# Output products of a hybrid mixer, on one Trainium2 core, written as twelve jobs of seven products

## The chip, the cores and the metric

The kernel is one program on one core of a Trainium2 chip (trn2). The metric is the device time of one execution in microseconds (us). Most executions of it agree within 0.3%, so differences of about 0.2% need several runs of each kernel.

## The reference

One layer of a decoder trunk on a sequence of 1024 tokens of width 1024, in fp32. What matters here is the middle of it, with what stands on both sides:

```python
h = x
h = h + 0.5 * swiglu(rms_norm(h, ffn1_norm), ffn1_w_in, ffn1_w_out)
h = h + hybrid_mixer(rms_norm(h, mix_norm), ...)
h = h + 0.5 * swiglu(rms_norm(h, ffn2_norm), ffn2_w_in, ffn2_w_out)
hn = rms_norm(h, ple_norm)
h = h + sigmoid(hn @ ple_w_gate) * (p @ ple_w_proj)      # then a last rms_norm

def hybrid_mixer(u, ...):
    # projections of u; branch A: gated linear attention (GLA), 4 heads of 256 columns
    y_gla = o @ gla_w_out                 # o: 1024 x 1024
    # branch B: indexer, top-k, latent attention, 8 heads of 128 columns
    y_dsa = od @ dsa_w_out                # od: 1024 x 1024
    return (sigmoid(g_A) * y_gla + sigmoid(g_B) * y_dsa) @ w_out
```

The change concerns the three products of 1024x1024 by 1024x1024 in the last lines: o by gla_w_out (wgo in the kernel), od by dsa_w_out (wdo), and the gated sum by w_out (wmo).

## The kernel before

Activations lie transposed: a tile is 128 columns of the model by 1024 tokens, and a 1024-wide matrix is 8 such tiles. An fp32 product is made of three passes on rounded values: every operand is split into a high part (a copy into the rounded type, on ScalarE, ACT) and a rest (value minus high part, on VectorE, DVE), and high by high, high by rest and rest by high are summed in PSUM. A matmul instruction takes a 128x128 block of weights and 512 tokens.

Two ways of multiplying stand in the kernel. The **plain** one is `dense` and `column` (L121 to L140): one output tile of 128 columns is 8 (blocks of the sum) x 2 (halves of the tokens) x 3 = 48 matmuls. The **seven products** (`_Job`, `seven`, L252) serve both feed-forwards: the weight block of a job and the tokens are cut in two each way, and seven products of sums of blocks (numbers 1, 5, 6, 3, 7, 2, 4 in the order SEVEN) take the place of eight. For 8 tiles of input and 2 of output, which is a job with 4 blocks of the sum (KP = 4), that is 7 x 4 x 3 = 84 matmuls where the plain way takes 96. It needs sums of weight blocks (`sums7`, four subtractions or additions of 128x512 for each job, on GpSimd, POOL, or on DVE for the jobs in the list `crowded`), the split of each of the seven weights (`headrest`, called by `split7`: 128x512, high part on ACT, rest on DVE), and operands that are sums of blocks of the tokens (tiles `xo`, read as pieces `b` of 128x512 from memory, high part on ACT, rest on DVE: `part`). PSUM has three banks for the seven products (table BANK: 1, 6, 7, 4 in the first, 5, 3 in the second, 2 in the third), so a product must wait until the product before it in its bank has been drained by `done`.

What sets the order: the feed-forwards issue everything through `_InOrder` engines, that is, in the order in which the Python code writes it. All else (the GLA, the top-k, the latent attention and `mixer_out`) is placed by a scheduler that sorts instructions for each engine. DMAs stand in the order of one queue, that of SyncE (SP).

A **transition** is a place in a feed-forward where the input of the jobs changes (from the gate and up projections to the output projection, and from one window of the output projection to the next): all 28 operand tiles (7 products by 4 blocks) are then read and split anew (`feed`, L398) while the last jobs of the old input and the first of the new are running.

Around the change:

- GLA (L1200 to L1211) ends with its output tiles `o`, split by ACT and POOL into a high part and a rest that go to memory as `d_og`, 2 tiles for each 128 columns, 4 DMAs for a head.
- Latent attention (L1336 to L1346) ends every block of 128 queries and pair of heads in PSUM (`pv`); ACT copies the high part (`oh`), DVE makes the rest (`ol`), and four DMAs of 64 KB store them as `d_od`. The gate projections are woven in between.
- `mixer_out` (L1362) reads them back (`reload`, 16 DMAs of 512 KB for each of the two) and makes 3 x 8 plain output tiles, 24 x 48 = 1152 matmuls: for each of wgo a gate multiplication (`y`), for each of wdo a gate multiplication, an addition to `y` on POOL and a split, for each of wmo the addition to the residual (`hm`, L1386).
- The second feed-forward (`ffn`, L301) then starts with one plain job (4 blocks of 24 matmuls, of which the first 72 matmuls are one run) whose operands are `hm` times a gain, split on ACT and DVE (`tile_alone`), and with the sum of squares of `hm` (`square`: ACT `sq`, DVE `ss`), from which `pstat` (a matmul with ones), `r` and the row factor `R` follow.

## Time and profile before

| | |
|---|---|
| median of 3 runs | 2715.18 us (2714.36 to 2715.75) |
| the profiled execution | 2716.55 us, span of its instructions 2714.8 us |
| mean granted TensorE clock | 0.979 of full speed |
| TensorE (PE) busy | 2599.2 us, 96% of the span, 12114 matmuls |
| VectorE (DVE) busy | 1809.0 us, 67% |
| ScalarE (ACT) busy | 1143.9 us, 42% |
| GpSimd (POOL) busy | 761.4 us, 28% |
| from the last latent matmul to the last matmul of `mixer_out` | 1647.3 to 1898.3 us of the span |

A matmul of 128x512 is shown with some 0.39 us, but matmuls overlap: what counts is the distance between two starts. The views name tiles without their numbers, `pd<-xo,w` is a matmul of the seven-product kind (or of the plain job of a feed-forward), `pd<-xh,wh` one of the plain kind. In the square brackets of a timeline stand the idle time of the engine just before the group and what ended it.

### The profile page before, as it was taken

The numbers are of one execution on the slowest core, as the hardware profiler recorded it, in microseconds if no ns is written. First come the engines' busy times: TensorE is split into PE (matmuls) and PEld (weight loads), VectorE is DVE, ScalarE is ACT, GpSimd is POOL, SyncE is SP. The second block draws the span as 40 slices with busy tenths as digits, with TensorE's granted clock in tenths as the row PEclk, the third lists the DMA queues.
The fourth block names the chain that finished last, engine by engine and source line by source line (L and its number), as shares of the span: only waits on it lengthen the run. The fifth ranks groups of instructions, "written<-read, shape, count | busy, mean of one in ns | idle before, by whom it ended". The sixth has DMA issues, their size and how long they took to land. (4 is left out here: it accounts for less than half of the span.)

```text
span 2714.8 us, 33415 instructions
## 1 busy us (share of the span) xinstructions
PE 2599.2 (96%) x12114; PEld 2156.9 (79%) x12114; DVE 1809.0 (67%) x3157; ACT 1143.9 (42%) x1814; POOL 761.4 (28%) x533
## 2 busy tenths in 40 slices
PE   8999999999999999898999999999799999999997
PEld 6788887777888878787778887887588888777786
DVE  7866658768568999986256663232876655866865
ACT  6443334435445555432257662121543333443542
POOL 1555553222002132223222220110165555322200
PEclk9999999999999999898999999999899999999998
DMA  3343336434323233231432266332134333643322
GB/s 133 132 148 129 116 124 243 168 115 143 95 78 109 98 120 140 78 132 63 168 105 98 91 211 232 111 116 86 47 133 150 130 112 124 244 167 114 119 94 85
DMA packets 129253, 346.21 MB, mean 128 GB/s; under 512 B 14488, under 2 KB 34880, under 8 KB 129088
## 3 DMA queue, kind: packets, MB, share of 16 engines
q1 hardware_dynamic: 129088, 344.08, 36.5%
q8 instruction: 95, 1.56, 0.2%
q14 instruction: 70, 0.57, 0.1%
HBM read 230.75 MB, written 110.65 MB: 126 GB/s over the span
## 5 line engine op out<-in xcount | busy, mean ns | idle before, releaser
L1399 PE MATMUL pd<-xo,w 128*128 128x512 f32 x5580 | 1296.2, 394 | 55.0 <-DVE xo L1399 14.7
L1399 PEld LDWEIGHTS pd<-xo,w 128*128 128x128 f32 x5580 | 1058.0, 190 | 291.7 <-DVE xo L1399 23.4
L139 PE MATMUL pd<-xh,wh 128*128 128x512 f32 x1346 | 533.7, 398 | 19.1 <-DVE z L1064 18.6
L139 PE MATMUL pd<-xl,wh 128*128 128x512 f32 x1346 | 531.0, 396 | 0.0
L139 PE MATMUL pd<-xh,wl 128*128 128x512 f32 x1346 | 451.2, 395 | 0.0
L1399 DVE TENSOR_TENSOR w<-wr,w 128x512 fp32r<-128x512 f32 (+1 forms) x272 | 213.3, 786 | 190.9 <-ACT w L1399 190.8
L139 PEld LDWEIGHTS pd<-xh,wh 128*128 128x128 f32 x1346 | 255.1, 190 | 73.4 <-DVE z L1064 17.6
L139 PEld LDWEIGHTS pd<-xl,wh 128*128 128x128 f32 x1346 | 255.4, 190 | 51.8 <-issue 1.0
L139 PEld LDWEIGHTS pd<-xh,wl 128*128 128x128 f32 x1346 | 254.2, 190 | 52.9 <-issue 0.5
L118 DVE TENSOR_TENSOR wl<-wr,wh 128x1024 fp32r<-128x1024 f32 (+1 forms) x106 | 125.4, 1183 | 213.0 <-PE pd L139 104.4
L1399 ACT ACTIVATE w<-wr 128x512 fp32r<-128x512 f32 (+1 forms) x272 | 161.9, 613 | 140.7 <-PE pd L1399 116.3
L117 ACT ACTIVATE wh<-wr 128x1024 fp32r<-128x1024 f32 (+1 forms) x106 | 101.8, 961 | 261.9 <-PE pd L139 226.8
L1399 POOL TENSOR_TENSOR g<-g,R 128x512 f32<-128x512 f32 x78 | 115.8, 1485 | 306.1 <-ACT g L1399 302.6
L1399 DVE TENSOR_TENSOR w<-ws,w 128x512 fp32r<-128x512 f32 (+1 forms) x195 | 177.4, 910 | 5.5 <-ACT w L1399 4.9
L1399 DVE TENSOR_TENSOR hr<-hr,pd 128x512 f32<-128x512 f32 x160 | 109.2, 683 | 102.4 <-PE pd L1399 102.3
L1399 ACT ACTIVATE w<-ws 128x512 fp32r<-128x512 f32 (+1 forms) x195 | 119.0, 611 | 97.9 <-PE pd L1399 73.2
L1399 POOL TENSOR_TENSOR ws<-wr 128x512 f32<-128x512 f32 (+1 forms) x59 | 97.5, 1653 | 209.6 <-DVE w L1399 209.6
L1399 ACT ACTIVATE g<-g 128x512 f32<-128x512 f32 (+1 forms) x85 | 55.1, 648 | 219.3 <-DVE g L1399 219.3
L1399 ACT ACTIVATE g<-pd 128x512 f32<-128x512 f32 x82 | 49.1, 598 | 169.7 <-PE pd L1399 169.7
L169 POOL TENSOR_TENSOR r<-r,mhalf 128x8 f32<-128x8 f32 (+1 forms) x11 | 17.2, 1565 | 366.5 <-DVE r L168 360.8
L1399 DVE TENSOR_TENSOR xo<-b,xo 128x512 fp32r<-128x512 f32 x138 | 109.7, 832 | 0.5 <-ACT xo L1399 0.5
L1133 POOL TENSOR_TENSOR g_e<-g_b 128x512 f32<-128x512 f32 x28 | 35.5, 1268 | 252.1 <-DVE g_b L1107 204.0
(272 smaller groups left out, 3417.7 us busy)
## 6 DMA issues: line engine op xcount, KB each, us to landing
wr<-wm SPq DMA_DIRECT2D x54, 512.0 KB, 3.4
wr<-w1i SPq DMA_DIRECT2D x44, 512.0 KB, 4.1
d_hid<-u SPq DMA_DIRECT2D x44, 512.0 KB, 4.8
d_ts<-ts SPq DMA_DIRECT2D x44, 512.0 KB, 2.6
wr<-w2i SPq DMA_DIRECT2D x44, 512.0 KB, 4.2
b<-d_ts SPq DMA_DIRECT2D x72, 256.0 KB, 3.1
b<-d_hid SPq DMA_DIRECT2D x66, 256.0 KB, 4.3
d_sp<-m SPq DMA_DIRECT2D x32, 256.0 KB, 3.1
```

Of the source, the lines that this page charges most:

```text
L117: (ac or nc.scalar).activation(wh, raw, AF.Copy)
L118: (eng or self.weng).tensor_tensor(wl, raw, F(wh), op=ALU.subtract)
L139: te.matmul(ps[h], ww[:, ks], v[:, h * 512:h * 512 + 512], start=first and ww is wh and v is xh, stop=last and ww is wl)
L169: nc.gpsimd.tensor_tensor(r, r, self.mhalf[:, :nb], op=ALU.pow)
L1133: nc.gpsimd.tensor_tensor(ev[:, :, :m], ref, bv[:, :, :m], op=ALU.subtract)
L1399: ins = getattr(self.eng, name)(*args, **kw)
```

## The change

`mixer_out` becomes twelve jobs of seven products, 4 for each of wgo, wdo, wmo, each with KP = 4 and two output tiles; they stand in one list with the jobs of the second feed-forward, use its buffers (they are reserved once for both) and are issued in written order. 12 x 84 = 1008 matmuls take the place of 1152.

- **What feeds them.** GLA stores seven pieces of 128x512 for each head (blocks and differences of blocks; 4 subtractions of 128x512 on POOL, 7 DMAs of 256 KB) and no longer splits its output. Latent attention stores, for the first four query blocks, ACT's copy `olo`, and for the last four one tile `pc` of five 128x128 blocks (2 copies on ACT, 4 subtractions of 128x128 on POOL, one DMA), both single-buffered; the DVE instruction `ol` is gone. The gated sum of jobs 4 and 5 is stored as finished pieces (`sums`), that of jobs 6 and 7 is made in place (`made`).
- **When.** `feed` is now a method: at most 6 pieces are asked for ahead. The first 12 of the 28 operand tiles of wgo are made before job 0, then 4 for each product. The feeds of wdo and wmo are spread over 13 products of jobs 3 and 4, and of jobs 7 and 8.
- **Into the feed-forward.** `ffn` is a generator; `tile_alone` and `square` of tiles 0 to 5 run inside job 11 (the last of wmo). The blocks of the plain job go through the queue of ready weights.
- **`crowded`.** The lists are given by hand now. In both feed-forwards the sums of weights of the jobs around the second and the third transition (jobs NF + 3, NF + 4, NF + 7, NF + 8) move from POOL to DVE; of the new jobs, 3, 4, 7, 8 and 11 have them on DVE.

The core of the diff:

```diff
-        self.next = (plain, 0)
+        self.next = (0, 0)
...
     def sums7(self, job, step, eng=None):
-        if job >= len(self.jobs):
+        if job >= len(self.jobs) or self.jobs[job].plain:
             return
...
-            self.ready.append(self.headrest(j.w[SEVEN[q]], j.n))
+            self.ready.append(self.headrest(j.blk[BLOCKS[q]] if j.plain else j.w[SEVEN[q]], j.n))
...
-        self.crowded = (NF - 1, NF)
...
             tile_alone(j)
             if plain == 1:
                 square(j, hs[j])
+                if j % 2:
+                    yield
...
-        hs = self.mixer_out(d, mg, xp, yp, hp)
...
-        self.start(self.products(a, "w2"), 1)
+        jobs = [_Job(a[w][n], KP) for w in ("wgo", "wdo", "wmo") for n in range(KP)]
+        jb = len(jobs)
+        self.start(jobs + self.products(a, "w2", 1),
+                   [3, 4, 7, 8, 11] + [jb + NF + i for i in (-1, 0, 3, 4, 7, 8)])
...
-                oh = u("e", dtype=FR)
-                ol = u("e", dtype=FR)
-                nc.scalar.activation(oh, o, AF.Copy)
-                nc.gpsimd.tensor_tensor(ol, o, F(oh), op=ALU.subtract)
-                nc.sync.dma_start(d["og"][2 * j], F(oh))
-                nc.sync.dma_start(d["og"][2 * j + 1], F(ol))
+                os[half] = o
+            ta, tb = u("e"), u("e")
+            for t, x, y in ((ta[:, lo], os[0][:, hi], os[0][:, lo]), (tb[:, hi], os[1][:, hi], os[0][:, hi]),
+                            (tb[:, lo], os[1][:, hi], ta[:, lo]), (ta[:, hi], os[1][:, lo], tb[:, lo])):
+                nc.gpsimd.tensor_tensor(t, x, y, op=ALU.subtract)
+            for p, t in ((1, os[0][:, lo]), (5, ta[:, lo]), (6, tb[:, lo]), (3, os[1][:, hi]), (7, tb[:, hi]),
+                         (2, os[1][:, lo]), (4, ta[:, hi])):
+                nc.sync.dma_start(d["og"][h][:, PIECE[p], :], t)
...
-                nc.scalar.activation(oh, pv[:, :256], AF.Copy)
-                nc.vector.tensor_tensor(ol, pv[:, :256], F(oh), op=ALU.subtract)
+                    nc.scalar.activation(ohi, pair_of[:, 0, :], AF.Copy)
+                    nc.scalar.activation(pc[:, 2, :], pair_of[:, 1, :], AF.Copy)
+                    for t, x, y in ((0, ohi, olo[:, 0, cs]), (1, pc[:, 2, :], pc[:, 0, :]), (3, pc[:, 2, :], ohi),
+                                    (4, olo[:, 1, cs], pc[:, 1, :])):
+                        nc.gpsimd.tensor_tensor(pc[:, t, :], x, y, op=ALU.subtract)
+                    nc.sync.dma_start(out[:, 1:6, cs], pc)
...
+        count = next(feeds[0])
+        for q in range(4):
+            self.sums7(0, q, self.ve if q else None)
+        while count < upto[0][0]:
+            count = next(feeds[0])
+        for q in range(AHEAD):
+            self.split7()
+        for job in range(12):
+            j.ops, j.done = ops[w], (gla_out, latent_out, added)[w](n)
+            for q in self.seven(job):
+                if n in (0, 3) and wi == (w if n == 0 else w + 1):
+                    turn += 1
+                    want = upto[wi][min(turn, len(upto[wi]) - 1)] if wi else min(28, 12 + 4 * turn)
+                    while count < min(28, want):
+                        count = next(feeds[wi])
...
+                if job == 11 and q in (0, 3, 5):
+                    next(ffn)
+        next(ffn)
```

Where the order moves, at three places. First the queue of SP between the latent attention and the output products. `d_od` is the attention's output in memory, `g` a gate, `xh`, `xl` the stored halves, `b` a piece of GLA's output `d_og`. Before:

```order
L1345 DMA d_od_147<-oh 128x128
L1345 DMA d_od_149<-oh 128x128
L1346 DMA d_od_148<-ol 128x128
L1346 DMA d_od_150<-ol 128x128
L1368 DMA g<-d_gate_103 128x1024
L1368 DMA g<-d_gate_104 128x1024
L1368 DMA g<-d_gate_105 128x1024
L1357 DMA xh<-d_od_135 128x1024
L1358 DMA xl<-d_od_136 128x1024
```

After:

```order
L1376 DMA d_od_194<-pc 128x5x128 x4
L313 DMA b<-d_og_187 128x512
L313 DMA b<-d_og_188 128x512
L313 DMA b<-d_og_189 128x512
L313 DMA b<-d_og_190 128x512
L313 DMA b<-d_og_187 128x512
L313 DMA b<-d_og_188 128x512
L313 DMA b<-d_og_189 128x512
L1393 DMA g<-d_gate_103 128x1024
L1393 DMA g<-d_gate_104 128x1024
L313 DMA b<-d_og_190 128x512
```

Before, GLA's output had been read by then, and the attention's output follows its last store; now GLA's output is read only behind the last store of the attention.

Second, DVE at the start of the output products. `w` is the rest of a weight, `xo` the rest of an operand tile, `b` the piece that it comes from, `y` an output. After (before, this place holds the rests `wl` of plain weights, each followed by two gate multiplications):

```order
L1547 TENSOR_TENSOR wr<-wr 128x512
L1547 TENSOR_TENSOR xo<-b,xo 128x512 x12
L1547 TENSOR_TENSOR w<-wr,w 128x512
L1547 TENSOR_TENSOR w<-ws,w 128x512 x3
L1547 TENSOR_TENSOR w<-wr,w 128x512
L1547 TENSOR_TENSOR xo<-b,xo 128x512 x4
L1547 TENSOR_TENSOR w<-wr,w 128x512
L1547 TENSOR_TENSOR xo<-b,xo 128x512 x4
L1547 TENSOR_TENSOR w<-wr,w 128x512
L1547 TENSOR_TENSOR xo<-b,xo 128x512 x4
```

Twelve operand tiles stand ahead of the first weight, and twelve more between the weights of the first products.

Third, DVE at the end of the output products. `hm` is the residual tile that the last products are added to, `xo<-hm,gains` the operand of the plain job of the feed-forward, `ss` the sum of squares. Before:

```order
L1386 TENSOR_TENSOR hm_15050<-pd,hm_15050 128x512 x2
L1386 TENSOR_TENSOR hm_15110<-pd,hm_15110 128x512 x2
L1386 TENSOR_TENSOR hm_15170<-pd,hm_15170 128x512 x2
L1399 TENSOR_TENSOR ss<-ss,sq 128x1024
L1399 SCALAR_TENSOR_TENSOR xo<-hm_14870,gains,xo 128x512 x2
L1399 TENSOR_TENSOR ss<-ss,sq 128x1024
L1399 SCALAR_TENSOR_TENSOR xo<-hm_14930,gains,xo 128x512 x2
L1399 TENSOR_TENSOR ss<-ss,sq 128x1024
```

After:

```order
L1547 TENSOR_TENSOR hm<-hm,pd 128x512
L1547 TENSOR_TENSOR w<-wr,w 128x512
L1547 SCALAR_TENSOR_TENSOR xo<-hm,gains,xo 128x512 x4
L1547 TENSOR_TENSOR ss<-ss,sq 128x1024
L1547 TENSOR_TENSOR hm<-hm,pd 128x512
L1547 TENSOR_TENSOR w<-wr,w 128x512
L1547 TENSOR_TENSOR hm<-hm,pd 128x512
L1547 TENSOR_TENSOR w<-wr,w 128x512
L1547 TENSOR_TENSOR hm<-hm,pd 128x512
L1547 TENSOR_TENSOR w<-wr,w 128x512
L1547 SCALAR_TENSOR_TENSOR xo<-hm,gains,xo 128x512 x2
L1547 TENSOR_TENSOR ss<-ss,sq 128x1024
```

The operands and squares of the feed-forward, which stood behind the last output tile, now stand between the drains (`hm<-hm,pd`) of the last job.

## Rows read from the trace of the kernel before

**Rows 1.** Page part 1: busy us (share of the span) and instructions of each engine

```profile
PE 2599.2 (96%) x12114; PEld 2156.9 (79%) x12114; DVE 1809.0 (67%) x3157; ACT 1143.9 (42%) x1814; POOL 761.4 (28%) x533
```

**Rows 2.** Stretches: us, then busy time (instructions) of each engine, PE's clock, DMA share, GB/s

```profile
1700.00:1750.00 50.00, 50.00 (x222) 41.42 (x221) 13.34 (x16) 6.38 (x6) 4.17 (x2) 1.00 0.33 106
1900.00:1910.00 10.00, 1.22 (x2) 0.50 (x2) 10.00 (x13) 9.10 (x14) 0.00 (x0) 0.67 0.13 52
1610.00:1620.00 10.00, 10.00 (x58) 8.69 (x56) 5.92 (x20) 4.65 (x10) 1.06 (x1) 1.00 0.79 286
1660.00:1670.00 10.00, 10.00 (x46) 8.28 (x45) 1.48 (x3) 0.20 (x1) 0.00 (x0) 1.00 1.03 413
```

**Rows 3.** PE's timeline around the output products: start us, us, instructions [idle before, releaser]

```profile
1647.30 0.40 PE L139 MATMUL pd<-xh,wh 128*128 128x512 f32 x1
...
1897.85 0.61 PE L139 MATMUL pd<-xh,wl 128*128 128x512 f32 x2
1904.82 1.22 PE L1399 MATMUL pd<-xo,w 128*128 128x512 f32 x2 [6.36 <-ACT w L1399]
1911.19 18.92 PE L1399 MATMUL pd<-xo,w 128*128 128x512 f32 x70 [5.15 <-DVE w L1399]
1929.94 1.84 PE L1399 MATMUL pstat<-ones,ss 128*128 128x1 f32 x16
...
1956.08 9.19 PE L1399 MATMUL pd<-xo,w 128*128 128x512 f32 x28 [4.77 <-ACT u L1399]
```

**Rows 4.** DVE and ACT, timeline and duration by form (ns min/median/max)

```profile
1907.99 1.40 DVE L1399 SCALAR_TENSOR_TENSOR xo<-hm,gains,xo 128x512 fp32r<-128x512 f32 x2
...
1910.45 2.49 DVE L1399 TENSOR_TENSOR w<-wr,w 128x512 fp32r<-128x512 f32 x4
...
L1399 ACT ACTIVATE xo<-b x138: 614/617/636, 435.6 to 2530.7; 128x512 fp32r<-128x512 f32 x138
```

**Rows 5.** Latent attention, ACT and POOL by form: duration, mean ns

```profile
L1341 ACT ACTIVATE oh<-pv x32: 358/378/388, 1397.6 to 1647.5; 128x256 fp32r<-128x256 f32 x32
...
L1294 POOL TENSOR_TENSOR nm<-bias,m 128x128 f32<-128x128 f32 x8 | 3.6, 460 | 61.0 <-DVE st L1306 31.6 <-DMA bias<-d_bias 29.4
```

**Rows 6.** DMAs: page part 6 (KB each, us from issue to landing), SP's timeline of issues

```profile
b<-d_ts SPq DMA_DIRECT2D x72, 256.0 KB, 3.1
...
1652.09 0.43 SPq L1357 DMA_DIRECT2D xh<-d_od  x1
```

**Rows 7.** PE's timeline at a transition of the second feed-forward

```profile
2366.14 1.76 PE L1399 MATMUL pd<-xo,w 128*128 128x512 f32 x6 [0.35 <-DVE xo L1399]
2369.14 1.67 PE L1399 MATMUL pd<-xo,w 128*128 128x512 f32 x6 [1.24 <-DVE xo L1399]
2373.12 1.01 PE L1399 MATMUL pd<-xo,w 128*128 128x512 f32 x3 [2.31 <-DVE xo L1399]
2374.81 64.72 PE L1399 MATMUL pd<-xo,w 128*128 128x512 f32 x278 [0.68 <-DVE xo L1399]
```

**Rows 8.** The same transition in stretches

```profile
2360.00:2370.00 10.00, 8.41 (x36) 6.24 (x35) 10.00 (x18) 5.34 (x10) 1.43 (x1) 1.00 0.94 346
2370.00:2380.00 10.00, 7.01 (x24) 4.99 (x23) 5.17 (x6) 2.48 (x5) 6.07 (x5) 0.83 1.04 399
```

**Rows 9.** DVE and POOL beside each other at the next transition

```profile
2427.37 1.28 DVE L1399 TENSOR_TENSOR xo<-b,xo 128x512 fp32r<-128x512 f32 x2
...
2429.90 2.39 DVE L1399 TENSOR_TENSOR xo<-b,xo 128x512 fp32r<-128x512 f32 x2
...
2430.06 1.67 POOL L1399 TENSOR_TENSOR ws<-wr 128x512 f32<-128x512 f32 x1 [10.98 <-DVE w L1399]
```

**Rows 10.** PE's first matmuls of the program

```profile
10.25 29.88 PE L1399 MATMUL pd<-xo,w 128*128 128x512 f32 x119 [0.22 <-DVE xo L1399]
```

**Rows 11.** What PE waited for in the GLA, 1100 to 1400 us

```profile
PE pd L139 <- DVE z L1064: 18.6, 6, 10.8
PE pq L1143 <- DVE g_X L1137: 8.6, 1, 8.6
```

More of the change, by code (lines that the diff above doesn't have):

```diff
@@ L188, in rsteps, with products @@
         nc.sync.dma_start(out[:, c0 * P:c1 * P], bass.AP(w.tensor, w.offset, [[0, P], [1, nb * P]]))
-    def products(self, a, w):
-        jobs = [_Job(a[w + "i"][f], KP) for f in range(NF)]
+    def products(self, a, w, plain):
+        jobs = [_Job(a[w + "i"][f], KP, f < plain) for f in range(NF)]
         for wi, (k0, k1) in enumerate(WINDOWS):
@@ L196, in products, with start @@
         return jobs
-    def start(self, jobs, plain):
-        self.jobs, self.plain = jobs, plain
+    def start(self, jobs, crowded):
+        self.jobs, self.crowded = jobs, crowded
         self.loaded, self.ready, self.todo = 0, [], collections.defaultdict(list)
-        self.next = (plain, 0)
+        self.next = (0, 0)
         self.load7()
-    def blocks(self, f, rows):
-        j = self.jobs[f]
-        for r in rows:
-            for c in (1, 2):
-                j.w[r, c] = self.headrest(j.blk[r, c], j.n)
     def load7(self):
@@ L299, in part, with place, m, feed @@
         return o
-    def ffn(self, hs, gain, gain2, d, keep, pool, hp, xa, follow, beside=None):
+    def place(self, p):
+        return (self.xa, "x") if p < 5 else (self.fp, "xb")
+    def m(self, name="m", dtype=F32):
+        return self.fp.tile([P, 512], dtype, tag="m", name=name)
+    def feed(self, items, get, put):
+        todo, asked = [(p, i, *get(p, i)) for p, i in items], []
+        def ask():
+            while todo and len(asked) < 6:
+                p, i, kind, t = todo.pop(0)
+                if kind == "whole":
+                    src, t = t, self.m("b")
+                    self.nc.sync.dma_start(t, src)
+                asked.append((p, i, kind, t))
+        ask()
+        yield 0
+        for c in range(len(items)):
+            ask()
+            p, i, kind, t = asked.pop(0)
+            if kind == "parts":
+                pool, tag = self.place(p)
+                o = pool.tile([P, T], FR, tag=tag, name="xo")
+                self.nc.sync.dma_start(F(o), t)
+            else:
+                o = self.part(t() if kind == "made" else t, *self.place(p))
+            put[p][i] = o
+            yield c + 1
+    def ffn(self, hs, gain, gain2, d, keep, jb, follow, beside=None):
         nc = self.nc
-        plain = self.plain
+        pool, hp, xa = self.fp, self.hp, self.xa
+        place, m = self.place, self.m
+        plain = sum(j.plain for j in self.jobs[jb:])
         lo, hi = slice(0, 512), slice(512, 1024)
-        self.crowded = (NF - 1, NF)
-        def place(p):
-            return (xa, "x") if p < 5 else (pool, "xb")
-        def m(name="m"):
-            return pool.tile([P, 512], F32, tag="m", name=name)
         xs = {p: [None] * KP for p in SEVEN}
@@ L360, in ffn @@
         if plain > 1:
-            self.blocks(0, (1, 2))
+            for _ in range(4):
+                self.split7()
         for j in range(KD):
-            if plain == 1 and j == KD - 2:
-                self.blocks(0, (1, 2))
             tile_alone(j)
@@ L559, in ffn @@
             pps.append({})
+            ws.append([self.ready.pop(0) for _ in BLOCKS])
             for a, h in ((0, 0), (0, 512), (1, 0), (1, 512)):
@@ L683, in run @@
         self.first = []
-        self.start(self.products(a, "w1"), 2)
+        self.start(self.products(a, "w1", 2), [NF + i for i in (-1, 0, 3, 4, 7, 8)])
         hs = []
@@ L805, in run, with end @@
         es.close()
+    def end(self, steps):
+        while True:
+            try:
+                next(steps)
+            except StopIteration as e:
+                return e.value
     def weave(self, first, second, share):
@@ new lines, in mixer_out, with gates @@
+        lo, hi = slice(0, 512), slice(512, 1024)
+        hp, fp = self.hp, self.fp
+        ops = [{p: [None] * KP for p in SEVEN} for _ in range(3)]
+        tt = self.ve.tensor_tensor
+        half = {1: (0, lo), 2: (0, lo), 5: (1, hi), 7: (1, hi), 6: (0, hi), 3: (0, hi), 4: (1, lo)}
+        ys = {}
+        def gates(w, n):
+            gs = [self.unit(fp, "t", "g") for _ in range(2)]
+            for i, g in enumerate(gs):
+                nc.sync.dma_start(g, d["gate"][8 * w + 2 * n + i])
+            return gs
@@ new lines, in mixer_out @@
+        feeds = [self.feed(every, lambda p, i: ("whole", d["og"][i][:, PIECE[p], :]), ops[0]),
+                 self.feed(every, lambda p, i: ("whole", d["od"][i][:, PIECE[p], :]), ops[1]),
+                 self.feed(sum(turns, []), get_y, ops[2])]
+        upto = ([12 + 4 * t for t in range(6)], [-(-28 * t // 13) for t in range(14)],
+                [sum(map(len, turns[:t])) for t in range(14)])
+        count = next(feeds[0])
+        for q in range(4):
+            self.sums7(0, q, self.ve if q else None)
```

306 lines of the change are left out of this document (183 added, 123 removed).

## The prediction, made before the changed kernel ran

> **What bounds the kernel now.** I began with the page's busy times: TensorE is busy for 96% of the span, DVE for 67% [rows 1]. So the time falls with the number of matmuls, and what PE waits for has to be read stretch by stretch. Second, the stretches: in a stretch of plain products without a wait, 222 matmuls start in 50.00 us at clock 1.00, which is 0.2252 us for one [rows 2]. Third, PE's timeline from the end of the latent attention to the second feed-forward. The output products run from 1647.30 to 1898.46 us (1897.85 + 0.61), 251.2 us [rows 3]. In the instruction order 48 of their 1152 matmuls stand among the attention's last ones, so 1104 lie in this stretch, and 1104 x 0.2252 = 248.6: before, almost nothing is lost there. The feed-forward behind it loses a lot: the next matmul starts at 1904.82, after 6.36 us of idle, the run of 70 at 1911.19, `pstat` at 1929.94, the fourth product of its second job at 1956.08 [rows 3]; the clock is down to 0.67 in the first 10 us [rows 2].
>
> A bound for what a written-order stretch loses comes from a transition of the second feed-forward: PE waits 0.35, 1.24, 2.31 and 0.68 us, each time for DVE's `xo` [rows 7]; in the 20 us there are 36 + 24 = 60 matmuls [rows 8] where 20 / 0.2252 = 88.8 fit, so 28.8 x 0.2252 = 6.5 us are lost, 4.6 of it in those waits and the rest with the clock, 0.83 in the second half.
>
> **The change part by part.** All terms are made against the profiled execution, 2716.55 us, which lies 1.4 above the median.
>
> Fewer matmuls. From the last latent matmul on, 12 x 84 = 1008 x 0.2252 = 227.0 us stand where there were 251.2: **-24.2**.
>
> The start. Before, PE went on at once at 1647.30 [rows 3], since GLA's output was on the chip. Now its first load stands in SP's queue behind the last store `pc`, and ACT and DVE have twelve operand tiles ahead of the first weight. On the path: two copies on ACT (378 ns for one of 256 columns, I take 0.8 with the wait), four subtractions on POOL, 460 ns for the nearest row of 128x128, 1.9 [rows 5]; the store's issue and the load's, 0.43 each, and 3.1 us to landing [rows 6]: 6.7 us. Behind the first piece come eleven of 262 KB and three gates of 524 KB, 4.46 MB, at 399 to 413 GB/s [rows 2, 8] 10.9 us, so the last piece is there at 17.6; then its rest, 0.6, and the first weight's head, 0.5: **+18.7**. Bounds: 14.5 if ACT sets the pace (12 x 0.62 [rows 4]), 23.4 if the loads run at the 286 GB/s of the attention's end [rows 2].
>
> The clock after that idle. The only row with so long a pause ahead of it is the program's start: 119 matmuls in 29.88 us [rows 10], where 119 x 0.2252 = 26.8: **+3** (0 to 4).
>
> Job 0. Its other 16 tiles come four to a product, three products ahead of their use; POOL's gate multiplications run beside them, and a weight load stands between pieces 23 and 24: **+2** (0 to 6).
>
> The two feeds of jobs 3, 4 and 7, 8. The order has 64 DVE instructions in each pair, and one takes 0.605 us back to back (four in 2.40, from 1910.45 to 1912.86 [rows 4]): 38.7 us, against 14 x 12 x 0.2252 = 37.8 of PE. So DVE and PE are level, and a loss of 1 is the least; the 6.5 of the feed-forward's transition, where the pieces come in bursts of four, is the nearest measured end. I take 5.5, nearer to that row since each wait there also lowered the clock: **+11** for both (2 to 13). Job 5, where a late drain of job 4 meets the first pieces of the gated sum: **+1**.
>
> The attention's end. The 48 matmuls that are gone from it are 10.8 us; from 1610 to 1620 PE was full [rows 2], so there they shorten it; further on the attention waits for its own DVE work and the gap stays. Against it stand `pc` and its first copy in one buffer each, a chain of ACT, POOL and a store for each block, 1.5. I take 5 - 1.5: **-3.5** (+1.5 to -10.8).
>
> The boundary to the feed-forward. Before, `pstat` starts 31.5 us after the last output matmul (1929.94 - 1898.46 [rows 3]). After, the operands of tiles 0 to 5 are ready; 72 matmuls are 16.2 us; of the last tile, DVE does the drain, a weight, two pairs of `xo` (1.33 each, 1907.99 to 1909.32 [rows 4]) and one `ss` of 1.13, so it is ready 0.6 after PE wants it: `pstat` 16.9 us after the end, 14.6 earlier. What follows, 26.1 us up to 1956.08 [rows 3], has the same instructions. But in job 11 two tiles' worth of `xo` and `ss`, 4.9 us, now stand in front of a drain, while the bank that it frees is wanted after a product of 2.7: 3.3 us in two waits, and 1 for the clock. **-10.3** (-6 to -14.6).
>
> Sums from POOL to DVE in the feed-forwards, at four transitions. Two `xo` take 1.28 us alone and 2.39 beside a POOL sum of 1.67 [rows 9]: 1.1 lost for a sum that costs DVE 0.6 if it does it itself. Eight sums a transition are at most 4 us of DVE's, where PE waits for DVE [rows 7]. I take 2 for each second transition and 0.75 for each third, which has fewer waits: **-5.5** (+2 to -11). The Trainium skill ("SBUF — State Buffer", Who interferes with whom) calls the port that DVE and GpSimd share an exclusive lock: the later of the two instructions blocks for the whole of the other. The row shows 1.1 of 1.67; by the rule a moved sum would give back 1.07, not 0.5, and this term would be about -11.
>
> GLA and latent work. ACT loses its copies, DVE 32 `ol` of 0.4, POOL's work stays about the same, SP has 28 DMAs in place of 16. PE is the bound there; but two waits, 18.6 us for `z` and 8.6 for `g_X` [rows 11], come from where the scheduler put DVE's instructions, and the order behind them differs now, without a rule for which way: **+1** (-8 to +10).
>
> Sum: -24.2 + 18.7 + 3 + 2 + 11 + 1 - 3.5 - 10.3 - 5.5 + 1 = -6.8, so 2709.8 for an execution like the profiled one, and **2708.4** by the median.
>
> **Rivals.** (1) *The loads set the pace* (slower). The start, job 0 and both feeds hang on pieces of 256 KB, and in the first feed 28 pieces, the gates and weights want 380 to 400 GB/s for 30 us. At 286 GB/s [rows 2] the start costs 4.7 more, job 0 3 more, a feed 2.5 more each: 12.7, so 2721. It decides below some 330 GB/s. Against it: 399 GB/s with pieces of that size [rows 8]. The Trainium skill ("DMA: Bandwidth & Descriptors", Bandwidth) asks for transfers of 1 MiB and more and gives HBM some 358 GB/s for a core; the rows show 413 [rows 2], and by the page's figure the first pieces would come 1.5 us later.
>
> (2) *The GLA's waits grow.* The 27 us of rows 11 are accidents of order; 10 more would give 2718. For it: seven stores and a POOL chain now hold GLA's buffers longer. Against it: DVE has less to do.
>
> (3) *The attention's end gives back all 10.8 and the feeds cost 2 each* (faster). -7.3 - 7 gives 2694. For it: PE is full there at times, and the pieces are spread over 13 products. Against it: DVE's 38.7 against 37.8.
>
> (4) *The lock rule holds*: 2703.
>
> (5) *The moved sums do nothing*, since POOL had them in time: +5.5, 2714. That the matmuls do not go is excluded: the order has 144 fewer.
>
> **How the numbers follow.** Forecast 45%, with a range of its own of 2701 to 2716; rival 1 15%, rival 2 13%, rival 3 17%, rival 4 6%, rival 5 4%. Some 0.2%, 5.4 us, is what a measurement of this kernel can tell from no change, so faster is below 2709.8, slower above 2720.6. Faster: 0.26 of the forecast, rivals 3 and 4: 0.49. Same: 0.19 of the forecast, rival 5, and 0.05 of rival 2: 0.28. Slower: rival 1 and the rest of rival 2: 0.23. For 8 in 10 the range reaches rival 3's time and beyond rival 1's: 2694 to 2723.
>
> **What would show it.** Between the last `pv` and the first `pd<-xo,w` 18 to 19 us of idle, ended by ACT or DVE and with DMA near 400 GB/s in it; a pitch of 0.225 in jobs 1, 2, 6, 9, 10; waits for `xo` of 4 to 6 us in each of jobs 3, 4 and 7, 8; `pstat` some 17 us after the last output matmul; in both feed-forwards fewer POOL `ws` and shorter waits at the second transitions. The sum is wrong if the attention's end moves by other than 3 to 4 us, if the GLA's two waits change, or if the idle at the start is above 23.

## The result: 18 us slower

| | before | after |
|---|---|---|
| median | 2714.77 us (2714.30 to 2715.75, 4 runs) | 2732.53 us (2732.25 to 2736.78, 4 runs) |
| the profiled execution, its span | 2716.55, 2714.8 us | 2732.25, 2730.5 us |
| TensorE's mean granted clock | 0.979 | 0.973 |

The ratio is 1.0069, with a 95% interval of 1.0051 to 1.0086. The forecast of 2708.4 and its range up to 2723 were both too low, and the sign was wrong. The page's busy times after, beside [rows 1]:

```profile
PE 2582.7 (95%) x11970; PEld 2135.1 (78%) x11970; DVE 1927.3 (71%) x3365; ACT 1215.0 (44%) x1984; POOL 798.5 (29%) x609
```

The 144 matmuls are gone and PE is busy 16.5 us less, yet the span is 15.7 longer. PE's timeline of the same stretch as [rows 3] tells where (start us, us, instructions, in brackets the idle time before and what ended it; L1547 is the line through which every in-order instruction passes):

```profile
1634.87 0.28 PE L1356 MATMUL pv<-a_pt,ckl 128*128 128x256 f32 x1
1654.82 17.63 PE L1547 MATMUL pd<-xo,w 128*128 128x512 f32 x70 [19.68 <-ACT w L1547]
1672.67 0.74 PE L1547 MATMUL pd<-xo,w 128*128 128x512 f32 x2 [0.23 <-DVE xo L1547]
1679.11 78.32 PE L1547 MATMUL pd<-xo,w 128*128 128x512 f32 x331 [5.71 <-DVE y L1547]
1759.34 2.36 PE L1547 MATMUL pd<-xo,w 128*128 128x512 f32 x6 [1.91 <-DVE xo L1547]
1763.20 3.33 PE L1547 MATMUL pd<-xo,w 128*128 128x512 f32 x6 [1.50 <-DVE xo L1547]
1768.13 20.56 PE L1547 MATMUL pd<-xo,w 128*128 128x512 f32 x77 [1.60 <-DVE xo L1547]
...
1802.99 27.08 PE L1547 MATMUL pd<-xo,w 128*128 128x512 f32 x108 [5.18 <-ACT acc L1547]
1831.23 5.73 PE L1547 MATMUL pd<-xo,w 128*128 128x512 f32 x24 [1.16 <-ACT acc L1547]
1840.22 5.00 PE L1547 MATMUL pd<-xo,w 128*128 128x512 f32 x21 [3.26 <-ACT w L1547]
...
1853.46 8.33 PE L1547 MATMUL pd<-xo,w 128*128 128x512 f32 x24 [3.77 <-DVE hm L1547]
...
1931.58 7.53 PE L1547 MATMUL pd<-xo,w 128*128 128x512 f32 x32 [1.55 <-DVE hm L1547]
...
1951.33 1.84 PE L1547 MATMUL pstat<-ones,ss 128*128 128x1 f32 x16
...
1977.47 2.93 PE L1547 MATMUL pd<-xo,w 128*128 128x512 f32 x6 [4.78 <-ACT u L1547]
```

After the idle start there are seven waits of 1.5 us or more up to 1853.46; before, the longest in the output products was 0.5 us. I count what a job loses as its length, from its first matmul to the next job's first, less 84 x 0.2252 = 18.92 us. Twelve jobs lose 52.6 us:

| jobs | forecast | lost |
|---|---|---|
| 0 | 5 (clock 3, job 2) | 10.6 |
| 3, 4 | 5.5 | 10.2 (0.4 + 9.8) |
| 5, 6 | 1 | 10.4 (2.5 + 7.9) |
| 7, 8 | 5.5 | 16.6 (5.1 + 11.5) |
| 1, 2, 9, 10 | 0 | 2.1 |
| 11 | 4.3 | 2.7 |

PE's own waits in that stretch are 29 us; the other 23 lie in matmuls that run, and some 16 of it is the clock. Stretches of the granted clock show it (columns as in [rows 2], the clock third from the right):

```profile
1679.00:1684.00 5.00, 4.89 (x12) 3.86 (x13) 2.25 (x3) 0.00 (x0) 4.88 (x4) 0.50 0.63 208
1760.00:1770.00 10.00, 6.83 (x15) 3.51 (x14) 9.62 (x12) 1.26 (x2) 3.26 (x2) 0.50 0.18 53
1803.00:1809.00 6.00, 6.00 (x16) 4.74 (x17) 2.96 (x5) 2.19 (x5) 0.00 (x0) 0.60 0.95 257
1853.00:1860.00 7.00, 6.54 (x17) 5.21 (x18) 5.90 (x10) 1.55 (x4) 0.00 (x0) 0.57 0.11 14
```

0.50 is the lower of the two levels, 1.2 GHz. It is granted for 3 to 14 us at a time, 44 us in the twelve jobs; 11 of them lie inside the waits, and the other 33 are matmuls at half speed, which is where the 16 come from. Not every wait brings it: the two of 1.16 and 3.26 us at 1831 to 1840 left the clock at 1.00.

By stages of the two profiled executions: up to the last latent matmul -12.3 us (1647.2 to 1634.9); from there to the last output matmul +48.3 (251.2 to 299.5, which is 19.7 of idle, 227.0 of matmuls and the 52.6); from there to the fourth product of the feed-forward's second job -14.5 (57.6 to 43.1); behind that -5.7. The sum is +15.8, the difference of the spans.

### The profile page after: what moved, and what is told of

Read it like the earlier page. It is cut to its first block, busy times and chain, and to the rows that moved or that the text cites. A ratio compares the mean times of both kernels' runs of the same rounds, so it can differ in the third digit from the quotient of the medians.

```text
span 2730.5 us, 33710 instructions
## 1 busy us (share of the span) xinstructions
PE 2582.7 (95%) x11970; PEld 2135.1 (78%) x11970; DVE 1927.3 (71%) x3365; ACT 1215.0 (44%) x1984; POOL 798.5 (29%) x609
## 4 chain that ended last, share of the span: by engine, by line
PE 38%; DVE 6%; issue 4%; DMA 2%; ACT 2%; POOL 0%; SPq 0%; DVEq 0%; POOLq 0%; ACTq 0%
PE pd L1547 25%; PE pd L141 9%; DVE xo L1547 2%; PE ptp L1347 1%; DVE w L1547 1%; DMA b<-d_og 1%; DVE hm L1547 1%; PE pv L1355 1%; PE pv L1354 1%; PE pqk L1305 1%; PE pqk L1306 1%; DMA b<-d_od 1%; PE pqk L1308 1%; PE pv L1356 1%; ACT xo L1547 0%
## 5 line engine op out<-in xcount | busy, mean ns | idle before, releaser
L1547 PE MATMUL pd<-xo,w 128*128 128x512 f32 x6588 | 1538.1, 395 | 90.3 <-ACT w L1547 22.9
L1547 PEld LDWEIGHTS pd<-xo,w 128*128 128x128 f32 x6588 | 1248.7, 190 | 377.8 <-DVE xo L1547 37.3
L1547 DVE TENSOR_TENSOR w<-wr,w 128x512 fp32r<-128x512 f32 (+1 forms) x320 | 247.6, 775 | 216.0 <-ACT w L1547 215.8
L141 PE MATMUL pd<-xh,wh 128*128 128x512 f32 x962 | 384.4, 400 | 9.1 <-DVE z L1079 9.1
L141 PE MATMUL pd<-xl,wh 128*128 128x512 f32 x962 | 382.7, 398 | 0.0
L141 PE MATMUL pd<-xh,wl 128*128 128x512 f32 x962 | 331.3, 396 | 0.0
L1547 ACT ACTIVATE w<-wr 128x512 fp32r<-128x512 f32 (+1 forms) x320 | 191.6, 614 | 151.3 <-PE pd L1547 122.1
L141 PEld LDWEIGHTS pd<-xh,wh 128*128 128x128 f32 x962 | 183.0, 190 | 47.2 <-DVE z L1079 10.2
L1547 POOL TENSOR_TENSOR ws<-wr 128x512 f32<-128x512 f32 (+1 forms) x59 | 100.0, 1694 | 388.7 <-DVE w L1547 388.7
L141 PEld LDWEIGHTS pd<-xl,wh 128*128 128x128 f32 x962 | 183.2, 190 | 37.3 <-issue 1.0
L141 PEld LDWEIGHTS pd<-xh,wl 128*128 128x128 f32 x962 | 182.1, 190 | 37.6 <-issue 0.5
L1547 DVE TENSOR_TENSOR w<-ws,w 128x512 fp32r<-128x512 f32 (+1 forms) x231 | 206.3, 894 | 5.5 <-ACT w L1547 4.9
L1547 POOL TENSOR_TENSOR g<-g,R 128x512 f32<-128x512 f32 x78 | 115.9, 1486 | 306.0 <-ACT g L1547 306.0
L1547 ACT ACTIVATE w<-ws 128x512 fp32r<-128x512 f32 (+1 forms) x231 | 140.9, 613 | 119.2 <-PE pd L1547 94.7
L1547 DVE TENSOR_TENSOR hr<-hr,pd 128x512 f32<-128x512 f32 x160 | 109.4, 684 | 93.5 <-PE pd L1547 93.2
L1547 ACT ACTIVATE g<-g 128x512 f32<-128x512 f32 (+1 forms) x85 | 55.1, 648 | 219.3 <-DVE g L1547 219.3
L1547 DVE TENSOR_TENSOR xo<-b,xo 128x512 fp32r<-128x512 f32 x201 | 139.8, 731 | 9.8 <-ACT xo L1547 9.7
L1547 ACT ACTIVATE xo<-b 128x512 fp32r<-128x512 f32 x201 | 120.1, 623 | 55.1 <-DMA b<-d_ts 26.0
L1547 ACT ACTIVATE g<-pd 128x512 f32<-128x512 f32 x82 | 49.0, 597 | 169.7 <-PE pd L1547 169.7
```

What stands on the lines that cost most here:

```text
L141: te.matmul(ps[h], ww[:, ks], v[:, h * 512:h * 512 + 512], start=first and ww is wh and v is xh, stop=last and ww is wl)
L1547: ins = getattr(self.eng, name)(*args, **kw)
```

## Experiments

"Lost" is counted as above. Where one run was made, only the stage is compared, since the stretch from the first feed-forward's end to the last latent matmul varies by 6 us between executions of the same instructions (960.8 to 966.5 in the eleven kernels that have the changed ones there). Kernels e4 and e11 are edits of the kernel before, all others of the changed one.

**e1: no loads behind the first twelve pieces.** In place of the other 16 pieces of wgo's feed and all 28 of wdo's, the operand tiles are made from a constant tile that lies on the chip, with the same two instructions.

```diff
+            elif kind == "fixed":
+                self.ac.activation(v[:, :4, :], src, AF.Copy)
+                self.ve.tensor_tensor(v[:, 4:, :], src, F(v[:, :4, :]), op=ALU.subtract)
...
-                 self.feed(every, lambda p, i: ("whole", d["od"][i][:, PIECE[p], :]), ops[1]),
+                 self.feed(every, lambda p, i: ("fixed", None), ops[1]),
```

> The changed kernel with the loads of 44 operand pieces left out: operand tiles 13 to 28 of the first input and all 28 of the second are split from a constant on the chip, so the outputs are not the layer's. All splits and their order stay. In the changed kernel job 0 loses 10.6 us against 84 x 0.2252, jobs 3 and 4 together 10.2. Theory 'order' (the drains on DVE and ACT stand in written order behind splits, and DVE has more to do than PE in jobs 3 and 4): jobs 3 and 4 still lose 7 or more; job 0, where splits wait for late loads, falls to 3 or less. Theory 'loads' (the transfers set the pace in all three places): jobs 3 and 4 fall below 3 and job 0 below 3.

2725.82 us. Job 0 lost 3.4 in place of 10.6 (3 or less was expected); jobs 3 and 4 still lost 9.8 in place of 10.2. So job 0's loss is mostly late loads, and that of jobs 3 and 4 is not the loads. A stretch of the changed kernel in job 0:

```profile
1658.00:1661.00 3.00, 3.00 (x14) 2.46 (x14) 1.14 (x2) 1.82 (x4) 2.92 (x2) 1.00 0.00 1
```

And the timelines of ACT, DVE and POOL in job 0:

```profile
1659.17 0.60 ACT L1547 ACTIVATE y<-pd 128x512 f32<-128x512 f32 x1 [2.85 <-PE pd L1547]
...
1671.26 0.63 ACT L1547 ACTIVATE xo<-b 128x512 fp32r<-128x512 f32 x1 [2.22 <-DMA b<-d_og]
...
1671.92 0.69 DVE L1547 TENSOR_TENSOR xo<-b,xo 128x512 fp32r<-128x512 f32 x1 [2.16 <-ACT xo L1547]
...
1673.73 4.63 DVE L1547 TENSOR_TENSOR xo<-b,xo 128x512 fp32r<-128x512 f32 x4
1678.29 0.68 DVE L1547 TENSOR_TENSOR y<-y,pd 128x512 f32<-128x512 f32 x1
...
1673.29 1.65 POOL L1547 TENSOR_TENSOR y<-y,g 128x512 f32<-128x512 f32 x1 [12.29 <-DVE y L1547]
1674.90 1.72 POOL L1547 TENSOR_TENSOR wr<-wr 128x512 f32<-128x512 f32 x1
```

The DMA moves 1 GB/s from 1658 to 1661 although nine pieces are still to come. Seven buffers hold pieces, and the next can be loaded only when tile 13 is split. Its copy stands in ACT's written order behind the first product's drain `y<-pd`, for which ACT waits 2.85 us. The lost time comes back at the end of the feed: ACT waits 2.22 us for a piece and DVE 2.16 for ACT; then four splits take 4.63 us, two of them 1.75 each beside the two POOL instructions; and the drain `y` behind them ends PE's 5.71. That the buffers are the reason is read from these rows, and no run gave the feed more of them.

**e3 and e5: begin with fewer tiles.** Eight tiles ahead of job 0 in place of twelve, and four.

```diff
-                    want = upto[wi][min(turn, len(upto[wi]) - 1)] if wi else min(28, 12 + 4 * turn)
+                    want = upto[wi][min(turn, len(upto[wi]) - 1)] if wi else min(28, 8 + 4 * turn)
```

> The changed kernel with 8 operand tiles in place of 12 ahead of the first weight, then 4 for each product as before. Theory 'order': the first product waits only because twelve splits stand ahead of its weight, so the idle of 19.7 us falls to about 15, and job 0's loss of 10.6 us does not grow: 4 to 8 us faster. Theory 'loads': the last tile lands no earlier, so what the start gains job 0 loses: within 2 us of the changed kernel.

> The changed kernel with 4 operand tiles in place of 12 ahead of the first weight, then 4 for each product. With 8 the idle fell from 19.7 to 16.0 us and job 0's loss stayed at 10.4. Theory 'order': idle 11 to 13 us; each product of job 0 then waits for four tiles whose splits and loads take some 3 us to its 2.7, loss of job 0 between 10 and 14, from the last latent matmul to the end of job 0 some 42 us (49.2 in the changed kernel, 45.3 with 8). Theory 'loads' (28 pieces and three gates come no faster): 45 us, what the idle loses job 0 gains.

e3: 2732.17 us, ratio 1.0065 (1.0052 to 1.0079); idle 16.0, job 0 lost 10.4: from the last latent matmul to job 0's end 45.3 us in place of 49.2, which the whole doesn't show. e5: 2746.33; the idle is down to 10.4, but job 0 lost 31.6. Both of e5's theories missed it. PE in e5:

```profile
1646.08 5.39 PE L1547 MATMUL pd<-xo,w 128*128 128x512 f32 x12 [10.39 <-ACT w L1547]
1653.20 0.50 PE L1547 MATMUL pd<-xo,w 128*128 128x512 f32 x1 [1.72 <-ACT xo L1547]
...
1660.10 0.50 PE L1547 MATMUL pd<-xo,w 128*128 128x512 f32 x1 [1.72 <-ACT xo L1547]
```

With no tile in hand, every product waits for its own: the drain of a product, a weight, four splits and the next product form a chain of 6.9 us (1653.20 to 1660.10) for 12 matmuls that need 2.7.

**e2: the gate multiplications of jobs 5 and 6 on DVE.**

```diff
-                    (self.ve if n in (0, 3) else self.pl).tensor_tensor(t, t, g, op=ALU.mult)
+                    self.ve.tensor_tensor(t, t, g, op=ALU.mult)
```

> The changed kernel with the gate multiplications of jobs 5 and 6 on DVE in place of POOL (6 instructions). Theory 'hop': in those jobs DVE's next instruction waits 1.4 us each time for POOL's result, DVE falls behind, and the split of the gated sum on ACT holds up a drain: jobs 5 and 6, which lose 2.5 and 7.9 us, lose 4 together, and the kernel gains 5 to 7 us. Rival 'DVE is full there anyway': six more instructions of 0.6 us on DVE, no gain or up to 4 us slower.

2730.42 us, ratio 1.0056 (1.0042 to 1.0070). Jobs 5 and 6 lost 5.7 in place of 10.4, job 8 9.6 in place of 11.5; all twelve 44.8 in place of 52.6. The whole program's times do not tell the two kernels apart. In the changed kernel's timelines, DVE, POOL and ACT ahead of the wait at 1802.99:

```profile
1795.95 1.76 DVE L1547 TENSOR_TENSOR y<-y,acc 128x512 f32<-128x512 f32 x1 [1.40 <-POOL acc L1547]
...
1801.11 0.68 DVE L1547 TENSOR_TENSOR ts<-y,ts 128x512 f32<-128x512 f32 x1
...
1794.62 1.29 POOL L1547 TENSOR_TENSOR acc<-acc,g 128x512 f32<-128x512 f32 x1 [4.00 <-DVE acc L1547]
...
1801.82 0.63 ACT L1547 ACTIVATE m<-ts 128x512 fp32r<-128x512 f32 x1 [7.03 <-DVE ts L1547]
1802.36 0.58 ACT L1547 ACTIVATE acc<-pd 128x512 f32<-128x512 f32 x1
```

DVE waits for POOL three times for 1.4 us; so its sum `ts` is late; ACT, in written order, stands 7.03 us on the copy `m<-ts`; and behind that copy stands the drain `acc<-pd` that PE needs. Without POOL in the chain PE's wait at that product falls from 5.2 to 2.4 us (e2's waits: sum, times, longest):

```profile
PE pd L1547 <- ACT acc L1547: 2.4, 1, 2.4
```

**e12: besides, the gated sum of job 4 stored unsplit and split when it is read**, so that no copy of `ts` stands ahead of job 6's drains on ACT.

```diff
-                if n:
+                if True:
                     nc.sync.dma_start(d["yy"][n][:, PIECE[p], :], src[p])
...
-            if n == 0:
-                return "parts", d["yp"][PIECE[p]]
-            if n == 1:
+            if n < 2:
```

> The kernel of e2 (gate multiplications of jobs 5 and 6 on DVE) with one more edit: the pieces of the first gated sum are stored whole, as those of the second are, and split when they are read in jobs 7 and 8, so ACT has no copy in job 5 that waits for DVE. In e2 jobs 5 and 6 still lose 1.2 and 4.4 us; there the copy of the last piece ends at 1803.36, 5.7 us after ACT was free, and the drain of job 6's first product stands behind it. Theory 'hop, second half': job 6 loses 1 or less, jobs 7 and 8, which get seven more splits, lose 2 to 5 more than the 14.5 of e2. Rival 'drain alone' (the product's own drain is late on its own account): job 6 still loses 3 or more.

2727.91 us. Job 6 lost 0.1, so its cause is as read. But jobs 7 and 8 lost 18.4 where e2 has 14.5: all twelve 44.2, no gain over e2. What left job 6 came back at the next feed.

**e9: no feeds.** Jobs 4 to 11 use the operand tiles of the first feed; the second and third feed's loads, copies, rests and block differences are left out.

```diff
-                 self.feed(every, lambda p, i: ("whole", d["od"][i][:, PIECE[p], :]), ops[1]),
-                 self.feed(sum(turns, []), get_y, ops[2])]
+                 self.feed(every, lambda p, i: ("same", ops[0]), ops[1]),
+                 self.feed(sum(turns, []), lambda p, i: ("same", ops[0]), ops[2])]
```

> The changed kernel with the operand tiles of the second and third input left out: jobs 4 to 11 multiply the tiles of the first input again, so loads, splits and block differences of those two feeds are gone and the outputs are not the layer's; weights, drains, gates and the stores of the gated sum stay. Theory 'DVE is full' (what jobs 3, 4 and 7, 8 lose is the DVE and ACT time of 28 splits each): jobs 3 and 4 together lose 1 or less in place of 10.2, jobs 7 and 8 together 4 or less in place of 16.6, job 9 nothing; job 6 still loses 7 to 8, since its wait comes from POOL's gate multiplications and the stored pieces. Rival 'drains' (PSUM banks and gate multiplications do it, not the feeds): more than half of the losses stay.

2705.73 us. Jobs 3, 4, 7 and 8 lost 0.1 each, 26.4 less than in the changed kernel; jobs 0 and 6 lost what they did (11.2, 7.6). So the two feeds cost 26 us. Even without them the program gains only 10 on the kernel before (2716.01 us beside this run), and none of the 10 in the output products: from the last latent matmul to the last output matmul it takes 271.8 us, 20 more than the 251.2 before.

**e6: wdo's tiles earlier**, three for each product in place of 28 over 13.

```diff
-        upto = ([12 + 4 * t for t in range(6)], [-(-28 * t // 13) for t in range(14)],
+        upto = ([12 + 4 * t for t in range(6)], [min(28, 3 * t) for t in range(14)],
```

> The changed kernel with the second feed (jobs 3 and 4) at 3 tiles a product, done after 10 products, in place of 28 over 13. Theory 'just in time': the last tiles of job 4 stand in DVE's order behind the drain of the product before the one that needs them, so its last products wait (2.3, 2.1 and 2.2 us); three products earlier these waits go and job 4 loses 3 to 6 us in place of 9.8. Theory 'DVE is full': DVE has 42.4 us of work against 37.8 of PE in these jobs, so the lag moves to the drains: job 4 still loses 8 or more, with waits for drains in place of tiles.

2736.57 us. Job 3 lost 5.3 and job 4 3.8: job 4 as 'just in time' has it, but the two together 9.1 in place of 10.2, only earlier. With e1 this says that DVE is full there. In the changed kernel's stretch DVE (third of the five) is busy 19.70 of 20 us:

```profile
1740.00:1760.00 20.00, 18.09 (x80) 14.62 (x79) 19.70 (x33) 15.41 (x28) 0.00 (x0) 1.00 0.98 375
```

From 1726.8 to 1769.8 DVE's 65 instructions take 42.4 us with 0.5 of idle, where PE has 37.8 of matmuls. Two causes stand in its timeline and POOL's: two pairs of `xo` that meet a POOL sum, and instructions that need the result of the one ahead and start 0.71 to 0.73 after it, where others start after 0.605.

```profile
1758.61 1.29 DVE L1547 TENSOR_TENSOR xo<-b,xo 128x512 fp32r<-128x512 f32 x2
...
1760.52 0.69 DVE L1547 TENSOR_TENSOR acc<-acc,g 128x512 f32<-128x512 f32 x1
1761.25 0.69 DVE L1547 TENSOR_TENSOR y<-y,acc 128x512 f32<-128x512 f32 x1
...
1762.46 2.37 DVE L1547 TENSOR_TENSOR xo<-b,xo 128x512 fp32r<-128x512 f32 x2
...
1762.62 1.65 POOL L1547 TENSOR_TENSOR ws<-wr 128x512 f32<-128x512 f32 x1 [39.95 <-DVE w L1547]
```

**e10: the sums of weights of jobs 3, 4, 7, 8 on POOL.**

```diff
-                   [3, 4, 7, 8, 11] + [jb + NF + i for i in (-1, 0, 3, 4, 7, 8)])
+                   [11] + [jb + NF + i for i in (-1, 0, 3, 4, 7, 8)])
```

> The changed kernel with the weight sums of jobs 3, 4, 7 and 8 back on POOL; those of the feed-forwards stay on DVE. DVE has 42.4 us of work in jobs 3 and 4, eight sums of 0.6 in it. Theory 'port' (a sum on POOL costs the DVE instruction beside it 1.1): jobs 3, 4 and 7, 8 lose 2 to 4 us more in each pair. Rival 'DVE's own count decides': each pair loses 3 to 5 less, since eight instructions are gone from a full DVE.

2738.11 us. Jobs 3 and 4 lost 11.6 (10.2 before), jobs 7 and 8 18.0 (16.6). DVE has eight instructions less in each pair of jobs and is not better off. Job 4 as a stretch, first of the changed kernel:

```profile
1742.09:1770.84 28.75, 23.67 (x86) 17.09 (x85) 27.27 (x41) 15.00 (x27) 3.26 (x2) 0.81 0.67 251
```

Then of e10:

```profile
1745.34:1775.76 30.42, 23.40 (x85) 16.69 (x84) 27.22 (x37) 14.95 (x27) 7.84 (x5) 0.84 0.71 262
```

37 DVE instructions are busy as long as 41 were, while POOL has 7.84 us in place of 3.26: what DVE saves, it loses beside POOL's sums. The sign is that of theory 'port', the size (1.4 in each pair) is neither theory's.

**e4: the moved sums alone**, in the kernel before.

```diff
-        self.crowded = (NF - 1, NF)
+        self.crowded = (NF - 1, NF, NF + 3, NF + 4, NF + 7, NF + 8)
```

> The kernel before with one part of the change alone: in both feed-forwards the weight sums around the second and the third transition (jobs NF + 3, NF + 4, NF + 7, NF + 8) on DVE in place of POOL. Theory 'sums' (a POOL sum beside a DVE split costs DVE 1.1 us, on DVE itself 0.6): 4 to 7 us faster than before, the waits of 2.2 and 0.8 us at the second transition gone or smaller. Rival 'the feed-forwards' gain in the changed kernel came from the new queue of plain blocks or the buffers': no difference from before.

2710.40 us (11 runs), ratio 0.9984 (0.9975 to 0.9993): -4.2 us against a median of 2714.57. At the second transition of the first feed-forward PE waits 2.19 us in the kernel before, for DVE's `hr`; in e4 this wait is gone, and those for `xo` behind it stay (0.84 and 0.73 us before; 0.64, 1.27 and 0.73 in e4). PE's timeline before:

```profile
541.27 14.68 PE L1399 MATMUL pd<-xo,w 128*128 128x512 f32 x55 [2.19 <-DVE hr L1399]
```

And in e4:

```profile
524.76 27.17 PE L1399 MATMUL pd<-xo,w 128*128 128x512 f32 x115
552.57 1.65 PE L1399 MATMUL pd<-xo,w 128*128 128x512 f32 x6 [0.64 <-DVE xo L1399]
```

**e7: the feed-forward's first steps behind job 11**, not inside it.

```diff
-                if job == 11 and q in (0, 3, 5):
-                    next(ffn)
         next(ffn)
```

> The changed kernel with the operands and squares of the second feed-forward's plain job not woven into job 11 but behind it, as the kernel before has them. Theory: job 11 loses 0 to 0.5 us in place of 2.7; the sums of squares' matmul stands 25 to 31 us behind the last output matmul in place of 16.9; the kernel gets 9 to 13 us slower, which is what the weaving brings. Rival: DVE and ACT would have done it in time anyway: less than 4.

2746.43 us, 14 more than the changed kernel, 8 of them ahead of the output products, where this edit changes nothing. At the boundary `pstat` starts 20.1 us after the last output matmul (16.9 in the changed kernel), while job 11 loses 0.1 in place of 2.7. Up to `pstat` the weaving is so worth 0.6 us. But the stretch behind `pstat`, up to the fourth product of the feed-forward's second job, is 31.2 us here, and 26.1 in the changed kernel and in each of the nine other edits of it. PE in e7:

```profile
1960.27 1.95 PE L1545 MATMUL pstat<-ones,ss 128*128 128x1 f32 x16 [1.45 <-DVE ss L1545]
...
1983.69 4.45 PE L1545 MATMUL pd<-xo,w 128*128 128x512 f32 x12 [6.15 <-ACT g L1545]
1991.49 3.78 PE L1545 MATMUL pd<-xo,w 128*128 128x512 f32 x8 [3.35 <-ACT u L1545]
```

So the weaving is worth 5.7 us in all, between theory and rival. The boundary (last output matmul to that fourth product) takes 57.6 us before, 51.3 without the weaving and 43.1 with it: 6.3 of its gain stay without the weaving, and there, as in e11 below, the weights of the plain job are ready ahead.

**e8: e2, e5 and e6 together.**

> The changed kernel with three edits together: gate multiplications of jobs 5 and 6 on DVE (mixer part 7.8 us shorter alone), 4 tiles ahead of the first weight, second feed done after 10 products. Theory 'order': the parts add, 15 to 22 us faster than the changed kernel, 2710 to 2717, on the kernel before. Theory 'DVE is full': only the gate's 5 to 8 and 4 of the start stay: 2720 to 2724.

2745.25 us, ratio 1.0103 (1.0082 to 1.0124): job 0 lost 31.8, as in e5, and both theories missed it.

**e11: the parts that help, in the kernel before.** The moved sums, and the weights of the plain job split after its third tile.

```diff
-        self.crowded = (NF - 1, NF)
+        self.crowded = (NF - 1, NF, NF + 3, NF + 4, NF + 7, NF + 8)
...
-            if plain == 1 and j == KD - 2:
+            if plain == 1 and j == 3:
                 self.blocks(0, (1, 2))
```

> Not the changed kernel: the kernel before with the weight sums of the feed-forwards' second and third transitions on DVE (alone 0.9984 of before) and one line of the boundary: the four weights of the plain job are split behind the operands of tile 3 in place of tile 6, so that PE needn't wait for them at 1911.19. In the changed kernel without the weaving, the sums of squares' matmul stood 20.1 us behind the last output matmul, in before 31.5, and there the weights stand ahead. Theory 'the weights' place makes the boundary': that distance falls from 31.5 to 24 to 27 and the kernel is 4 to 7 us faster than with the sums alone, 2703 to 2707. Rival 'the tiles' pace of 2.46 us sets it': less than 2 us.

2705.58 us (2704.12 to 2706.03, 5 runs), ratio 0.9960 (0.9947 to 0.9974): faster than both kernels. PE's timeline at the boundary, beside [rows 3]:

```profile
1899.26 0.61 PE L139 MATMUL pd<-xh,wl 128*128 128x512 f32 x2
1899.71 0.61 PE L1399 MATMUL pd<-xo,w 128*128 128x512 f32 x2
1905.22 1.22 PE L1399 MATMUL pd<-xo,w 128*128 128x512 f32 x2 [4.90 <-DVE w L1399]
...
1923.60 1.84 PE L1399 MATMUL pstat<-ones,ss 128*128 128x1 f32 x16
```

Of the two waits of 6.36 and 5.15 us ahead of the run of 70 matmuls one of 4.90 is left, and `pstat` starts 23.7 us after the last output matmul in place of 31.5, a little sooner than expected.

## Why the prediction was wrong

Step by step, with the forecast's term first:

- **Matmuls, -24.2:** right, by count.
- **The start, +18.7:** 19.7. Right in size and in mechanism: with eight tiles (e3) it is 16.0, with four (e5) 10.4, so twelve pieces and their splits set it. The DMA moved 377 GB/s while it ran (the row below), so rival 1, with its 286 GB/s, didn't hold for the start.

```profile
1640.00:1655.00 15.00, 0.18 (x1) 0.18 (x2) 8.87 (x15) 8.28 (x14) 0.00 (x0) 0.50 1.01 377
```

- **Clock after the idle and job 0, +5:** 10.6. The clock behind the idle start cost 1.4 of the forecast 3 (it rises again 2.9 us after the first matmul). The term of job 0 was mis-sized: I took four tiles for each product, three products ahead, as enough, and didn't ask which buffer the next piece needs and what stands ahead of the instruction that frees it. e1 shows 7.2 of it as late pieces. By the rows shown under e1 what makes them late is not the rate of loads but the three us in which none may start; no run tests that by itself.
- **The feeds, +11:** 26.4 (e9). This is the step that failed most. I had DVE's count right (65 instructions, 64 forecast) and priced each at its best, 0.605 us, so that 38.7 stood against PE's 37.8; it took 42.4. Then I took the loss at a feed-forward's transition as the nearest measured end, 6.5, and chose 5.5. There 4.6 us of waits cost 1.9 more with the clock; here, in jobs 3, 4, 7 and 8, 15.7 us of waits went with 11 more in the matmuls, 7 of it by the clock. My reason for 5.5, that each wait there lowered the clock, was not in the rows either: [rows 8] have one stretch at 0.83. In jobs 3 and 4 DVE is the bound (e1, e6). In jobs 7 and 8 it was not separated: DVE is busy 17 of the 20 us from 1830, ACT stands four times, 14.6 us in all, on DVE's `y` with weights behind it, and the DMA is full until 1840, then all but idle (the stretches below), so that the loads don't set job 8's longest wait, 3.77 us at 1853.46. That the whole loss goes with the feed is shown (e9); which of the three sets the rest is open.

```profile
1830.00:1835.00 5.00, 3.84 (x18) 3.12 (x18) 3.93 (x8) 2.68 (x5) 0.00 (x0) 1.00 1.04 422
1835.00:1840.00 5.00, 1.96 (x9) 1.30 (x7) 4.30 (x7) 2.48 (x5) 0.00 (x0) 1.00 1.03 407
...
1845.00:1850.00 5.00, 4.19 (x16) 2.74 (x15) 4.13 (x7) 1.59 (x3) 0.00 (x0) 1.00 0.01 3
```

- **Job 5, +1:** 10.4 over jobs 5 and 6. Missed. I looked at the tiles that job 6 uses and not at what its own drains go through: POOL, DVE and ACT in turn, on three engines that may not overtake. e2 and e12 show the chain link by link.
- **The attention's end and the GLA, -2.5:** from the first feed-forward's end to the last latent matmul 970.8 us in three executions of kernels with the old instructions there, 963.2 in eleven with the new: -7.6. The size is nearer to rival 3 than to the forecast, and the place was wrong for both. Up to the first matmul of the latent attention (`pqk`) the mean fell from 700.6 to 689.8 us; from there to the last it rose from 270.2 to 273.4. In either kernel 528 plain matmuls stand in the attention, so the 48 are missing ahead of it, where also the wait for `z` fell from 18 us to 9. What each of the two is worth was not separated, and the second is what I had named as a sign that the sum is wrong. The single buffers did cost something: PE waits 2.5 us for `pc`.
- **The boundary, -10.3:** -14.5 and 2.7 in job 11, so -11.8. `pstat` came 16.9 us after the last output matmul, as forecast. But I had put the gain down to the weaving alone; e7 shows 5.7 for it, and 6.3 that stay without it, from weights that are ready earlier.
- **The sums, -5.5:** -4.2 by e4. At the second transitions the wait of 2.19 us is gone in both feed-forwards of the changed kernel, and shorter ones for `xo` stay; in PE's timeline of the first, 330 matmuls run through the place of it:

```profile
473.24 77.82 PE L1547 MATMUL pd<-xo,w 128*128 128x512 f32 x330 [2.32 <-DVE xo L1547]
```

Rival 4 (-11) is out by that interval, and rival 5 (no effect) as well. A pair of `xo` beside one POOL sum takes 2.37 us in place of 1.29 (e6), so 1.08 of the sum's 1.65 are lost. But this is no sign against the rule behind rival 4. The sum runs until 1764.27, and the pair ends at 1764.83, 0.56 us behind it; in [rows 9] it is 0.56 us too; and in the changed kernel's trace 211 of the 244 DVE instructions of 128x512 that start inside such a POOL instruction and outlast it end 0.54 to 0.56 us behind its end. So DVE waits until the POOL instruction has ended. The Trainium skill ("SBUF — State Buffer", Who interferes with whom) calls the port an exclusive lock, held for a whole instruction while the other engine is blocked, and the trace agrees. What was wrong is my price: all of the 1.67 is lost only by an instruction that starts together with the sum; one that starts later loses the rest of it.

The forecast's terms for the jobs add up to 21.3 us, 52.6 were lost; this 31 is more than the whole error of 24, and the stretches ahead of them and behind the boundary gave 5 and 3 back. The range missed because the feeds' upper bound (13 for both) was a row of another place, and because no rival had the feeds' cost on DVE in it: rival 1 looked for the slower side at the loads.
